# Recurrent heads issued one head ahead of the attention heads in a hybrid decoder block

## Chip, core, metric

The kernel runs on one core of a Trainium2 chip. The metric is the device time of one execution in microseconds (us). It is compared with the kernel before on the same inputs: 1024 tokens, model width 1024, one layer, float32.

## What is computed

One decoder block. The normed input `h` goes through one wide projection; part of it feeds an RWKV-7 recurrence (8 heads of 64), part a differential attention (4 heads, two score maps each), part the two gates of the merge. The merged result passes `w_out`, a residual, and then a PEER expert layer: for each token 128 rows of a table `u` and 128 rows of a table `v` are chosen by product keys.

```python
z = h @ w_in
zs, zq, zk, zv, zg = split(z)
ya = rwkv7_time_mix(token_shift(zs))         # a scan over time, per head
yb = diff_attention(zq, zk, zv)              # (softmax1 - lam*softmax2) @ v, ALiBi, causal
ga, gb = split(zg)
x = x + (sigmoid(ga) * (ya @ proj_a) + sigmoid(gb) * (yb @ proj_b)) @ w_out
h2 = rmsnorm(x)
ids, gates = product_key_topk(h2)            # 128 experts per token
act = gelu(u_tab[ids] . h2) * gates
x = rmsnorm(x + sum(act * v_tab[ids]))
```

## The kernel before

The 1024 tokens are worked in two groups of 512 (`GROUPS`, L25). For each group a generator `mix` (L245) makes the time mixing, the attention, the merge and the residual; `pick` (L679) scores the product keys. The recurrence is done for two RWKV heads at a time, so `rwkv(h)` with h = 0 to 3 is called a recurrent head here. It is written in chunks of 64 tokens: a decay scan (`G`, L304), products per chunk (`MB`, L335), a triangular inverse that goes out to memory and back (`m_s`, `z_s`, L369 to L385, then `XT`, L405), transfer matrices (`Pd`, L440), eight serial state steps (`sn` and `st`, L468 and L469), and the output `ysb`, finished at L482 and stored to `y_s`. `attention(h)` (L508) makes the scores of four tiles of 128 queries, the softmax and the values, and ends with `oT` (L590), also stored to `y_s`. In the second group it reads the first group's keys and values back (`ko`, `vo`, L513). `rkv(h)`, `att_in(h)` and `gate_in(i)` are column blocks of the projection, 24 matmuls each (`z`), whose weights are split into two parts on ACT (`whi`, L154) and DVE (`wlo`, L155). `fill()` (L611) puts gate columns between the attention tiles; `NG` says how many belong to which head.

The merge (L627) reads the eight `y_s` blocks back (`yld`), splits them, and makes for each of eight output blocks `d` the two halves i = 0 (recurrent) and i = 1 (attention): the product with `proj` (`pj`), times the gate (`sgm`), and the sum (`mg`, L643, L645). Then `w_out` and the residual (`x`, L669).

The expert layer is done in two ways. For the first group's four chunks of 128 tokens, `choose` (L712) makes `ids`, and `peer` (L807) gathers the rows: 128 gathers of `u` and 128 of `v` for each chunk, 1024 in all, each a POOL-issued indirect DMA into one of five `uv` buffers and one DVE instruction on 128x1024 elements (L815 or L822). For the second group, `gates` and `ahead` prepare dense gate tables and `dense` (L861) runs through all 128 blocks of 128 experts, here called dense heads: on DVE each has one `gw` multiplication at L885, and the results in PSUM are added up at L926.

All this is handed to a tile scheduler in the order in which it is written: what comes earlier in the text has priority, and the scheduler fixes for each engine one order of instructions before the program runs. The gathers of `peer` are written last (L954), so they fill what the scheduler holds to be free places. On the chip each engine works through its list in that order; an instruction that waits holds back all behind it. The four `choose` calls of the first group are handed over at the `yield`s of the second group's `mix` (L932 to L935, `CHO`).

Of the kernel before, what the change touches and what calls it, by code (L numbers as in the profile page):

```python
# [9 lines left out]
F32R = mybir.dt.float32r  # L10
# [4 lines left out]
OP = mybir.AluOpType  # L15
# [22 lines left out]
NG = (2, 3, 3, 8)  # L38
# [10 lines left out]
def body(ctx: ExitStack, tc: tile.TileContext, ins, out, dbg=None):  # L49
    nc = tc.nc  # L50
# [194 lines left out]
    def mix(gi, t0, W):  # L245
# [241 lines left out]
        def att_in(h):  # L487
            slope = 2.0 ** (-2 * (h + 1))
            b = zt(14 + h)
            qT = at("qT")[:, :W]  # L490
            nc.scalar.activation(qT, b, AF.Copy, scale=0.125 / slope)
            b = zt(18 + h)
            kT = at("kTn")[:, :W]
            nc.scalar.activation(kT, b, AF.Copy)
            b = zt(22 + h)
            t = at("zvT")[:, :W]
            nc.scalar.activation(t, b, AF.Copy)
            b2 = abank("vtr")[:, :W]
            for a in range(TT):
                nc.tensor.transpose(b2[:, a * P:(a + 1) * P], t[:, a * P:(a + 1) * P], ident)  # L500
            vn = at("vn")[:, :W]
            nc.scalar.activation(vn, b2, AF.Copy)
            if t0 + W < T:
                nc.sync.dma_start(ins["k_s"][h, :, t0:t0 + W], kT)
                nc.sync.dma_start(ins["v_s"][h, :, t0:t0 + W], vn)
            return qT, kT, vn

        def attention(h, qT, kT, vn, fill):  # L508
            slope = 2.0 ** (-2 * (h + 1))
            segs = []  # L510
            if t0:
                ko, vo = at("ko")[:, :t0], at("vo")[:, :t0]
# [1 line left out]
                nc.sync.dma_start(vo, ins["v_s"][h, :, 0:t0])  # L514
                segs.append((0, t0, ko, vo))
            segs.append((t0, t0 + W, kT, vn))
            bo = obank("oT")[:, :W]
            def scores(a):

# [82 lines left out]
        nc.scalar.activation(lo_[0:64, :], lo_[0:64, :], AF.Tanh)  # L602
        nc.scalar.activation(gl, gl, AF.Sigmoid)
        show("lora", lo_, (slice(None), slice(t0, t0 + W)))
        zz, q = rkv(0), att_in(0)
        yield
        order = iter(range(16))
        for h in range(4):
            left = [NG[h]]

            def fill():  # L611
                if left[0]:
                    left[0] -= 1
                    gate_in(next(order))

            rwkv(h, *zz)
            if h < 3:
                zz = rkv(h + 1)
            attention(h, *q, fill)
            if h < 3:  # L620
                q = att_in(h + 1)
            while left[0]:
                fill()
            yield


        yh, yl, mcat = [], [], []  # L627
        for k in range(8):
            y = at("yld")[:, :W]
            nc.sync.dma_start(y, ins["y_s"][gi, k, :, :W])  # L630
            yh.append(rt_("yh", F32R))
            yl.append(rt_("yl", F32R))
            split(y, yh[k], yl[k])
        mg = [r2("mg") for _ in range(4)]
        for d in range(8):
            m = []
            for i in range(2):
                sgm = at("sgm")[:, :W]
                nc.sync.dma_start(sgm, ins["g_s"][gi, 8 * i + d, :, :W])
                b = zbank("pj")[:, :W]  # L640
                wmul(b, ins["proj"][d, i:i + 1], lambda k: yh[4 * i + k], lambda k: yl[4 * i + k], 4)
                t = mg[d // 2][:, d % 2 * 512:d % 2 * 512 + W] if i == 0 else sgm
                nc.vector.tensor_tensor(t, sgm, b, op=OP.mult)  # L643
                m.append(t)
            nc.vector.tensor_tensor(m[0], m[0], m[1], op=OP.add)  # L645
            show("mrg", m[0], (d, slice(None), slice(t0, t0 + W)))
            mcat.append(m[0])
        mh, ml = [], []
        for m in mcat:
            mh.append(rt_("mh", F32R))  # L650
# [380 lines left out]
```

## Times and profile before

| | us |
|---|---|
| median of 3 runs (lowest, highest) | 3510.96 (3509.01, 3511.16) |
| the profiled execution, its own time | 3513.99 |
| span of its profile | 3512.2 |
| PE busy in the span | 3085.0 |
| DVE busy | 2876.8 |
| ACT busy | 1412.5 |
| POOL busy | 1334.3 |

The profile is of one execution. Its time is 1.8 us over its span and 3.0 us over the median. PE is TensorE, DVE VectorE, ACT ScalarE, POOL GpSimd; SP issues most DMAs. Matmul ends are modelled, so PE's busy share says less than the distance between the starts of matmuls. The program has stages with different limits, so that shares over the whole span say little and the stretches must be read one by one.

### The profile page before, as it was taken

How to read it: one execution, taken by the hardware profiler on the slowest of the kernel's cores; microseconds unless marked ns; L12 is line 12 of the kernel's file. 1: busy time of each engine (PE TensorE's matmuls, PEld its weight loads, DVE VectorE, ACT ScalarE, POOL GpSimd, SP SyncE). 2: the span in 40 equal slices, each digit the busy share in tenths (PEclk: the TensorE clock that was granted, in tenths of full speed). 3: DMA queues.
4: the chain of work that ended last, by engine and by line, in shares of the span. 5: the costliest groups of instructions: out<-in, count | busy, mean ns of one | idle time of the engine just before them, and what ended most of it. 6: DMA issues, size and time to landing. Idle time of an engine off the chain costs nothing. (4 is left out here: it accounts for less than half of the span.)

```text
span 3512.2 us, 51039 instructions
## 1 busy us (share of the span) xinstructions
PE 3085.0 (88%) x17382; PEld 2404.1 (68%) x17382; DVE 2876.8 (82%) x6546; ACT 1412.5 (40%) x2634; POOL 1334.3 (38%) x1036
## 2 busy tenths in 40 slices
PE   6999998999778965889888689999989999999996
PEld 5777776777555754667666468777767777777775
DVE  4655557977978777999888679998989998988999
ACT  3444434443424331334999543333323333333332
POOL 0000000024553355421122426665555665655664
PEclk9999999998888886999989799999999999999998
DMA  4222454256675688864668999999999999999997
GB/s 128 75 74 72 122 159 160 77 174 220 227 252 185 221 284 291 308 199 133 198 209 276 308 343 343 351 358 350 356 345 345 352 353 349 367 348 339 354 351 279
DMA packets 407525, 898.69 MB, mean 256 GB/s; under 512 B 69024, under 2 KB 140000, under 8 KB 403168
## 3 DMA queue, kind: packets, MB, share of 16 engines
q0 software_dynamic: 147456, 536.94, 43.4%
q1 hardware_dynamic: 259808, 358.49, 30.4%
q8 instruction: 137, 2.24, 0.3%
q14 instruction: 124, 1.02, 0.1%
HBM read 829.22 MB, written 66.07 MB: 255 GB/s over the span
## 5 line engine op out<-in xcount | busy, mean ns | idle before, releaser
L793 POOL DMA_INDIRECT uv<-u,ids x512 | 655.2, 1280 | 1255.3 <-DVE uv L815 626.6
L793 POOL DMA_INDIRECT uv<-v,ids x512 | 677.9, 1324 | 519.2 <-DVE acc L822 372.4
L822 DVE SCALAR_TENSOR_TENSOR acc<-uv,act,acc 128x1024 f32<-128x1024 f32 x512 | 655.4, 1280 | 72.2 <-DMA uv<-v,ids 65.7
L815 DVE SCALAR_TENSOR_TENSOR uv<-uv,hb 128x1024 f32<-128x1024 f32 x512 | 617.4, 1219 | 87.3 <-DMA uv<-u,ids 84.5
L154 ACT ACTIVATE whi<-wraw 128x512 fp32r<-128x512 f32 x552 | 339.0, 627 | 595.2 <-PE z L170 207.1
L155 DVE TENSOR_TENSOR wlo<-wraw,whi 128x512 fp32r<-128x512 f32 x552 | 374.5, 686 | 132.5 <-ACT whi L154 124.9
L169 PE MATMUL ua<-fh,whi 128*128 128x512 f32 x1024 | 419.7, 410 | 61.5 <-ACT ye L905 39.9
L170 PE MATMUL ua<-fl,whi 128*128 128x512 f32 x1024 | 417.3, 408 | 0.0
L176 ACT ACTIVATE ah<-gw 128x512 fp32r<-128x512 f32 x128 | 80.8, 632 | 727.0 <-DVE gw L885 723.1
L180 PE MATMUL yk<-vh,ah 128*128 128x512 f32 x768 | 307.0, 400 | 25.8 <-ACT ah L176 24.8
L182 PE MATMUL yk<-vh,al 128*128 128x512 f32 x768 | 308.3, 401 | 6.8 <-DVE al L177 5.8
L181 PE MATMUL yk<-vl,ah 128*128 128x512 f32 x768 | 306.0, 398 | 5.8 <-DVE vl L177 5.8
L173 PE MATMUL ua<-fh,wlo 128*128 128x512 f32 x1024 | 269.7, 402 | 23.6 <-DVE wlo L155 23.6
L169 PEld LDWEIGHTS ua<-fh,whi 128*128 128x128 f32 x1024 | 201.1, 196 | 112.9 <-ACT ye L905 45.1
L169 PE MATMUL z<-hh,whi 128*128 128x512 f32 x672 | 274.8, 410 | 1.0 <-ACT whi L154 1.0
L173 PE MATMUL z<-hh,wlo 128*128 128x512 f32 x672 | 275.1, 410 | 0.7 <-DVE wlo L155 0.7
L170 PE MATMUL z<-hl,whi 128*128 128x512 f32 x672 | 275.3, 410 | 0.0
L844 PE MATMUL gb<-oh,ohg 128*128 128x128 f32 x1024 | 228.3, 344 | 40.3 <-ACT ohg L843 37.8
L173 PEld LDWEIGHTS ua<-fh,wlo 128*128 128x128 f32 x1024 | 193.5, 191 | 73.0 <-DVE wlo L155 31.4
L844 PEld LDWEIGHTS gb<-oh,ohg 128*128 128x128 f32 x1024 | 168.0, 212 | 103.1 <-ACT ohg L843 64.4
L843 ACT ACTIVATE ohg<-ohb,sl 128x128 f32<-128x128 bf16 x512 | 231.2, 560 | 2.0 <-DVE ohb L838 2.0
L170 PEld LDWEIGHTS ua<-fl,whi 128*128 128x128 f32 x1024 | 201.0, 196 | 44.3
(321 smaller groups left out, 5739.8 us busy)
## 6 DMA issues: line engine op xcount, KB each, us to landing
wraw<-ut SPq DMA_DIRECT2D x256, 256.0 KB
vraw<-v SPq DMA_DIRECT2D x256, 256.0 KB
wraw<-w_in SPq DMA_DIRECT2D x168, 256.0 KB
gd_s<-st SPq DMA_DIRECT2D x16, 2048.0 KB
gt<-gd_s SPq DMA_DIRECT2D x32, 1024.0 KB
wraw<-wq SPq DMA_DIRECT2D x64, 256.0 KB
g_s<-sgo SPq DMA_DIRECT2D x32, 256.0 KB
wraw<-proj SPq DMA_DIRECT2D x32, 256.0 KB
```

What stands on the lines that cost most here:

```text
L154: nc.scalar.activation(hi, raw, AF.Copy)
L155: nc.vector.tensor_tensor(lo, raw, hi.bitcast(F32), op=OP.subtract)
L169: nc.tensor.matmul(o, hi, xh(k), start=(k == 0), stop=False)
L170: nc.tensor.matmul(o, hi, xl(k), start=False, stop=False)
L173: nc.tensor.matmul(o, lo, xh(k), start=False, stop=(k == n - 1))
L180: nc.tensor.matmul(o, ah, bh, start=first, stop=False)
L181: nc.tensor.matmul(o, ah, bl, start=False, stop=False)
L182: nc.tensor.matmul(o, al, bh, start=False, stop=last)
L793: nc.gpsimd.indirect_dma_start(out=t, out_offset=None, in_=ins[src], in_offset=bass.IndirectOffsetOnAxis(ap=ids[:, j:j + 1], axis=0))
L815: nc.vector.scalar_tensor_tensor(u, u, 1.0, hb, op0=OP.mult, op1=OP.mult, accum_out=act[:, j:j + 1])
L822: nc.vector.scalar_tensor_tensor(acc, v, act[:, j:j + 1], acc, op0=OP.mult, op1=OP.add)
L844: nc.tensor.matmul(b[:, k:512:4], o3[:, k], o1[:, k], start=True, stop=True)
```

## The change

Two things are written in another order.

First, the loop over heads runs five times. In round h it hands over `rwkv(h)` and the next head's columns `rkv(h + 1)`, and then the attention of head h - 1 with its gate columns. Before, `rwkv(h)`, `rkv(h + 1)` and `attention(h)` came together, so a recurrent head now stands ahead of the attention of the head before it, and attention 3 with its eight gate columns stands alone at the end. The `yield`s, and with them the `choose` calls, come after attention 0 to 3 as before. The reads of `ko` and `vo` move from `attention` into `att_in`, one head earlier.

Second, the merge takes the half i = 0 of all eight blocks first, with the four recurrent `yld` blocks, and then the half i = 1 with the four of the attention. The same products and sums are made; nothing is added or left out.

```diff
@@ -503,10 +503,6 @@
             if t0 + W < T:
                 nc.sync.dma_start(ins["k_s"][h, :, t0:t0 + W], kT)
                 nc.sync.dma_start(ins["v_s"][h, :, t0:t0 + W], vn)
-            return qT, kT, vn
-
-        def attention(h, qT, kT, vn, fill):
-            slope = 2.0 ** (-2 * (h + 1))
             segs = []
             if t0:
                 ko, vo = at("ko")[:, :t0], at("vo")[:, :t0]
@@ -514,6 +510,10 @@
                 nc.sync.dma_start(vo, ins["v_s"][h, :, 0:t0])
                 segs.append((0, t0, ko, vo))
             segs.append((t0, t0 + W, kT, vn))
+            return qT, segs
+
+        def attention(h, qT, segs, fill):
+            slope = 2.0 ** (-2 * (h + 1))
             bo = obank("oT")[:, :W]
             def scores(a):
 
@@ -602,49 +602,55 @@
         nc.scalar.activation(lo_[0:64, :], lo_[0:64, :], AF.Tanh)
         nc.scalar.activation(gl, gl, AF.Sigmoid)
         show("lora", lo_, (slice(None), slice(t0, t0 + W)))
+
         zz, q = rkv(0), att_in(0)
         yield
         order = iter(range(16))
-        for h in range(4):
-            left = [NG[h]]
-
-            def fill():
-                if left[0]:
-                    left[0] -= 1
-                    gate_in(next(order))
-
-            rwkv(h, *zz)
+        left = [0]
+
+        def fill():
+            if left[0]:
+                left[0] -= 1
+                gate_in(next(order))
+
+        for h in range(5):
+            if h < 4:
+                rwkv(h, *zz)
             if h < 3:
                 zz = rkv(h + 1)
-            attention(h, *q, fill)
-            if h < 3:
-                q = att_in(h + 1)
-            while left[0]:
-                fill()
-            yield
+            if h:
+                left[0] = NG[h - 1]
+                attention(h - 1, *q, fill)
+                if h < 4:
+                    q = att_in(h)
+                while left[0]:
+                    fill()
+            if h:
+                yield
 
 
         yh, yl, mcat = [], [], []
-        for k in range(8):
-            y = at("yld")[:, :W]
-            nc.sync.dma_start(y, ins["y_s"][gi, k, :, :W])
-            yh.append(rt_("yh", F32R))
-            yl.append(rt_("yl", F32R))
-            split(y, yh[k], yl[k])
         mg = [r2("mg") for _ in range(4)]
-        for d in range(8):
-            m = []
-            for i in range(2):
+        for i in range(2):
+            for k in range(4 * i, 4 * i + 4):
+                y = at("yld")[:, :W]
+                nc.sync.dma_start(y, ins["y_s"][gi, k, :, :W])
+                yh.append(rt_("yh", F32R))
+                yl.append(rt_("yl", F32R))
+                split(y, yh[k], yl[k])
+            for d in range(8):
                 sgm = at("sgm")[:, :W]
                 nc.sync.dma_start(sgm, ins["g_s"][gi, 8 * i + d, :, :W])
                 b = zbank("pj")[:, :W]
                 wmul(b, ins["proj"][d, i:i + 1], lambda k: yh[4 * i + k], lambda k: yl[4 * i + k], 4)
-                t = mg[d // 2][:, d % 2 * 512:d % 2 * 512 + W] if i == 0 else sgm
-                nc.vector.tensor_tensor(t, sgm, b, op=OP.mult)
-                m.append(t)
-            nc.vector.tensor_tensor(m[0], m[0], m[1], op=OP.add)
-            show("mrg", m[0], (d, slice(None), slice(t0, t0 + W)))
-            mcat.append(m[0])
+                m = mg[d // 2][:, d % 2 * 512:d % 2 * 512 + W]
+                if i == 0:
+                    nc.vector.tensor_tensor(m, sgm, b, op=OP.mult)
+                    continue
+                nc.vector.tensor_tensor(sgm, sgm, b, op=OP.mult)
+                nc.vector.tensor_tensor(m, m, sgm, op=OP.add)
+                show("mrg", m, (d, slice(None), slice(t0, t0 + W)))
+                mcat.append(m)
         mh, ml = [], []
         for m in mcat:
             mh.append(rt_("mh", F32R))
```

What the scheduler makes of it is read from the orders of the two programs. `z` is a column block of the projection, `bg` the last product of a recurrent head, `am` the first products of the next one; lines behind L602 stand six lines later in the changed program.

**PE, first group, between recurrent heads 0 and 1.** Before, from `bg` of head 0 on, columns of the projection stand between all steps of the next head; the piece begins

```order
L481 MATMUL bg<-gl,lora 128x512
L589 MATMUL hb<-ident,rsw 128x128
L173 MATMUL z<-hh,wlo 128x512
L169 MATMUL z<-hh,whi 128x512
L170 MATMUL z<-hl,whi 128x512
```

and now

```order
L481 MATMUL bg<-gl,lora 128x512
L235 MATMUL hs<-blk,sq 128x2 x4
L242 MATMUL hb<-ident,rb 128x128 x4
L289 MATMUL bu<-wlal,lora 128x512
L293 MATMUL ba<-wlal,lora 128x512
L318 MATMUL bb<-av,blk 128x512
L332 MATMUL am<-KR,bT 64x128 x16
L332 MATMUL am<-KR,kT 64x128 x16
```

From `Pd` of head 0 to `am` of head 1 there were 109 matmuls of `z` (36 up to `bg`, 38 up to `bu`, 35 up to `am`); now there are none. They stand behind the last recurrent head instead: between its `bg` and the first `w_out` product there were 17, now 166.

**DVE, second group, end of recurrent head 3.** Before, `ysb` of head 3 and `oT` of attention 3 stood side by side, and the merge followed:

```order
L590 SCALAR_TENSOR_TENSOR oT<-oT,sub_105,hb 128x512
L482 TENSOR_TENSOR ysb<-ysb,bg 128x512
L177 TENSOR_TENSOR yl<-yld,yh 128x512
L822 SCALAR_TENSOR_TENSOR acc<-uv,act,acc 128x1024 x5
L177 TENSOR_TENSOR yl<-yld,yh 128x512
L822 SCALAR_TENSOR_TENSOR acc<-uv,act,acc 128x1024
```

Now this `oT` is that of attention 2, and the choice of the last chunk, gate columns and gathers follow:

```order
L590 SCALAR_TENSOR_TENSOR oT<-oT,sub_105,hb 128x512
L482 TENSOR_TENSOR ysb<-ysb,bg 128x512
L750 CAST d_11708<-ch 128x128
L828 SCALAR_TENSOR_TENSOR acc<-uv,act,acc 128x1024
L751 TENSOR_SCALAR d_11708<-d_11708 128x128
L155 TENSOR_TENSOR wlo<-wraw,whi 128x512
L752 SCALAR_TENSOR_TENSOR d_11708<-d_11708 128x128
```

Attention 3 and its gate columns come after that, ahead of the merge. Counted on DVE in the two orders, the gathers that stand ahead of certain places are:

| gathers ahead of | before | changed |
|---|---|---|
| first `ids` of the second group's mix | 0 | 0 |
| `ysb` of recurrent head 3 | 215 | 219 |
| first `mg` of the merge | 221 | 251 |
| first residual `x` | 255 | 282 |
| first dense head | 366 | 395 |
| dense head 64 | 667 | 694 |
| dense head 124 of 0 to 127 | 998 | 1024 |
| first `accd` (L926) | 1019 | 1024 |

**DVE, end of the program.** Before, gathers stand among the last sums:

```order
L822 SCALAR_TENSOR_TENSOR acc<-uv,act,acc 128x1024
L926 TENSOR_TENSOR accd<-accd,yk 128x512
L822 SCALAR_TENSOR_TENSOR acc<-uv,act,acc 128x1024
L926 TENSOR_TENSOR accd<-accd,yk 128x512 x5
L822 SCALAR_TENSOR_TENSOR acc<-uv,act,acc 128x1024
L907 TENSOR_TENSOR accd<-accd,ye 128x512 x2
```

and now the last four dense heads and the sums stand without any:

```order
L891 TENSOR_TENSOR gw<-gw,gt 128x512
L177 TENSOR_TENSOR al<-gw,ah 128x512
L913 TENSOR_TENSOR accd<-accd,ye 128x512
L177 TENSOR_TENSOR vl<-vraw,vh 128x512
L913 TENSOR_TENSOR accd<-accd,ye 128x512
L932 TENSOR_TENSOR accd<-accd,yk 128x512 x6
```

## Rows read from the trace of the kernel before

**Rows 1.** Page, part 4: the chain that ended last, by engine.
```profile
issue 20%; POOL 15%; DMA 7%; ACT 2%; DVE 1%; PE 1%; POOLq 0%; DVEq 0%; ACTq 0%
```

**Rows 2.** Windows: us, busy of PE, PEld, DVE, ACT, POOL (instructions), PE clock, DMA share, GB/s.
```profile
94.00:449.00 355.00, 349.28 (x3608) 263.71 (x3607) 208.63 (x671) 164.57 (x294) 0.46 (x4) 0.99 0.29 86
...
145.00:194.00 49.00, 46.74 (x451) 34.85 (x442) 28.88 (x94) 19.64 (x34) 0.11 (x1) 0.97 0.22 71
...
750.00:908.00 158.00, 128.51 (x1058) 95.15 (x1058) 135.15 (x402) 54.42 (x91) 75.49 (x59) 0.82 0.72 237
908.00:1070.00 162.00, 127.20 (x1072) 95.25 (x1072) 136.22 (x396) 57.11 (x94) 82.36 (x58) 0.85 0.70 229
1070.00:1235.00 165.00, 149.45 (x1161) 116.44 (x1162) 129.96 (x353) 69.21 (x111) 61.17 (x47) 0.89 0.64 207
1235.00:1369.00 134.00, 80.16 (x883) 63.80 (x882) 107.35 (x188) 31.78 (x59) 76.00 (x60) 0.75 0.82 279
1369.00:1475.00 106.00, 89.02 (x362) 68.81 (x361) 90.56 (x108) 26.19 (x43) 44.66 (x38) 0.92 0.91 316
...
2026.00:3430.00 1404.00, 1323.74 (x5533) 1051.48 (x5534) 1267.64 (x1761) 461.34 (x839) 819.39 (x625) 0.98 0.96 350
3430.00:3484.00 54.00, 51.27 (x213) 40.73 (x213) 52.04 (x58) 14.45 (x26) 35.16 (x29) 0.97 0.86 295
```

**Rows 3.** Timeline of DVE, first group: start us, us, instruction [idle before].
```profile
145.31 0.42 DVE L440 TENSOR_TENSOR Pd<-Pp,eyec 128x256 f32<-128x256 f32 x1 [2.67 <-PE Pp L430]
...
193.75 0.69 DVE L335 TENSOR_TENSOR MB<-am,mask 128x512 f32<-128x512 f32 x1 [0.22 <-PE am L332]
...
448.44 0.68 DVE L482 TENSOR_TENSOR ysb<-ysb,bg 128x512 f32<-128x512 f32 x1
...
460.75 0.68 DVE L643 TENSOR_TENSOR mg<-sgm,pj 128x512 f32<-128x512 f32 x1
...
543.40 0.68 DVE L669 TENSOR_TENSOR x<-x,xo 128x512 f32<-128x512 f32 x1
```

**Rows 4.** Timeline of PE, first group: five projection matmuls in a row, first and last.
```profile
83.72 0.39 PE L170 MATMUL z<-hl,whi 128*128 128x512 f32 x1
...
84.63 0.39 PE L173 MATMUL z<-hh,wlo 128*128 128x512 f32 x1
```

**Rows 5.** Timeline of DVE, second group: recurrent head 3, first merge sum, first residual.
```profile
1368.50 0.68 DVE L482 TENSOR_TENSOR ysb<-ysb,bg 128x512 f32<-128x512 f32 x1
...
1387.80 0.69 DVE L643 TENSOR_TENSOR mg<-sgm,pj 128x512 f32<-128x512 f32 x1 [3.32 <-DMA sgm<-g_s]
...
1475.35 0.68 DVE L669 TENSOR_TENSOR x<-x,xo 128x512 f32<-128x512 f32 x1
```

**Rows 6.** Groups of DVE, 750 to 1475 us: busy us, mean ns | idle before.
```profile
L822 DVE SCALAR_TENSOR_TENSOR acc<-uv,act,acc 128x1024 f32<-128x1024 f32 x127 | 162.5, 1279 | 18.4 <-DMA uv<-v,ids 17.5
L815 DVE SCALAR_TENSOR_TENSOR uv<-uv,hb 128x1024 f32<-128x1024 f32 x128 | 154.6, 1215 | 8.6 <-DMA uv<-u,ids 8.6
...
L815 DVE DVE_READ_ACCUMULATOR uv<-uv,hb 128x1 f32 x128 | 10.2, 80 | 0.0
```

**Rows 7.** Waits of DVE and PE, 700 to 1480 us: us in total, times, longest us.
```profile
DVE yl L177 <- ACT yh L176: 5.7, 1, 5.7
...
DVE mg L643 <- DMA sgm<-g_s: 3.3, 1, 3.3
...
PE sc L528 <- DMA ko<-k_s: 18.7, 3, 8.3
```

**Rows 8.** Timeline of DVE, end: `gw` of dense head 124, first sum, last gathered row.
```profile
3443.46 0.68 DVE L885 TENSOR_TENSOR gw<-gw,gt 128x512 f32<-128x512 f32 x1
...
3483.52 0.68 DVE L926 TENSOR_TENSOR accd<-accd,yk 128x512 f32<-128x512 f32 x1
...
3493.47 1.28 DVE L822 SCALAR_TENSOR_TENSOR acc<-uv,act,acc 128x1024 f32<-128x1024 f32 x1
```

**Rows 9.** Page, part 3: the queue of the 1024 gathers: packets, MB, share.
```profile
q0 software_dynamic: 147456, 536.94, 43.4%
```

## Prediction

> **What bounds the kernel now.** I read the chain of waits first. It ends in the gathers: "issue" and POOL hold a third of the span, and no other engine comes near [rows 1]. That says where the program ends, not what each stage waits for, so I went on to the windows, cut at the places that the order names [rows 2].
>
> The reader is to see three regimes there. In the first group's heads (94 to 449 us) PE is busy for 349.28 of 355 us at a clock of 0.99, and there are no gathers: PE is the limit. In the second group's mix (750 to 1475 us) the granted clock falls to between 0.75 and 0.92 (means of its two levels, 1.2 and 2.4 GHz) and PE has gaps. DVE, which now also carries the gathers, is busy for 135.15 + 136.22 + 129.96 + 107.35 + 90.56 = 599.2 of 725 us; 125.8 us are idle. It is nearest to the limit, held back by the recurrence. From 2026 us on (dense heads beside gathers) the DMA engines are busy for 0.96 at 350 GB/s and DVE for 1267.64 of 1404 us: this stage is full.
>
> The time at the end is therefore the start of the dense stage plus what that stage has left. The change can act on the first group's mix, on the second group's mix, and on the tail through the gathers that the mixes leave over.
>
> **First group.** No work is added. What moves is the filling: between `Pd` of head 0 and `am` of head 1 there were 109 projection matmuls and now there are none. That stretch took 193.75 - 145.31 = 48.4 us [rows 3], and PE was busy for 46.74 of 49 us there [rows 2]. Five projection matmuls in a row start 0.91 us apart from first to last, so one costs 0.91 / 4 = 0.23 us [rows 4]; 109 of them are 25 us. If the steps of the recurrence are quick without them, the stretch takes 48.4 - 25 = 23 us and the 25 us are paid later: a sum of 0. If the recurrence itself needs the 48 us, 25 us are added. On the other side, `ysb` of head 3 and the first merge sum stood 460.75 - 448.44 = 12.3 us apart [rows 3], a wait for stores and reads back, which 166 matmuls now cover. The term lies between -12 and +25 us. I take 0, because the row of that stretch shows PE full and not waiting.
>
> **Second group.** DVE carries the same instructions as before and more gathers: 282 instead of 255 stand ahead of the first residual, 27 more. One is a row of `v` at 1.28 us and 26 are rows of `u` at 1.215 + 0.080 us [rows 6], together 1.28 + 26 x 1.295 = 35 us. If the idle time stays at 125.8 us, the stretch grows by 35 us. Two waits go, since the recurrent half of the merge finds its inputs stored long before: `yl` 5.7 and `mg` 3.3 us, 9 us in all [rows 7]. The earlier reads of `ko` and `vo` take three PE waits of 18.7 us away [rows 7]; I cost that at nothing, as DVE and not PE is the fuller engine in this stretch. If that cover goes, they are a gain of up to 18.7 us. The two reads stand earlier on SP's queue; they are the same 256 KB each, and two more buffers are held for one head. The gap of 1387.80 - 1368.50 = 19 us ahead of the merge [rows 5] is filled by the choice of the last chunk, gate columns and attention 3, which were ahead of it before: work moved, not saved. The eight gate columns and their `wlo` move with it, at the same count.
>
> So the term is +35 - 9 = +26 us. The bounds: all 27 gathers fall into idle time, -9 us; or the idle share becomes that of the worst quarter, 1070 to 1235 us, with 35.0 of 165 us idle [rows 2]: (599.2 + 35) / 0.788 = 805 us, +80 us. The best quarter (22.9 of 158 us idle) gives 742 us, +17 us. I take +26 us, near the best quarter.
>
> **From the residual to the dense heads.** 111 gathers stood in it, now 113: the same work, hidden in the same places. I cost it at 0; two gathers more would be 2.6 us.
>
> **Tail.** By bytes it should shrink a lot. A gather moves 536.94 / 1024 = 0.524 MB [rows 9], 29 fewer are 15.2 MB, and at 350 GB/s that is 43 us. But the order does not let the tail run ahead. Up to dense head 124 it holds 998 - 366 = 632 gathers before and 1024 - 395 = 629 now, at the same steady mixture. Three gathers less are -4 us. Only the last four dense heads lose theirs. They took 3483.52 - 3443.46 = 40 us [rows 8], with DVE busy for 52.04 of 54 us and 213 matmuls starting in that time [rows 2]. Without 21 gathers DVE has 27 us less to do, PE is next, and 213 x 0.23 = 49 us instead of 54 make 4 us of the 40. After the first `accd` five gathers go, 5 x 1.28 = -6 us. Together -14 us. Bounds: -37 us if DVE alone set the end (29 x 1.28), 0 if the closing stores do.
>
> The DMA share is 0.64 to 0.91 in the mix and 0.96 in the tail [rows 2], and the change moves gathers from the fuller stage into the less full one; were the tail paid by bytes, the sum would be 0 + 26 - 43 = -17 us. That is a rival below. The Trainium skill, page Perfetto Trace Analysis, section Optimization Strategy, speaks for that rival: a kernel whose contended engine changes from stage to stage may gain when the stages are interleaved. By the rule this change should gain; by the counts of the order the tail keeps its pace and the sum stays at +12 us.
>
> **Sum.** 0 + 26 + 0 - 14 = +12 us on the profiled execution's 3513.99 us. That execution is 3.0 us over the median of the runs, so against 3510.96 us the forecast is 3523 us, slower by 0.3%. About 0.2%, 7 us, is what a measurement of this kernel can tell from no change.
>
> **The rivals.**
>
> *The mix swallows the gathers (faster).* The place is DVE between 750 and 1475 us. It has 125.8 us of idle time, and the recurrence, now ahead of the attention, leaves gaps of its own for gathers. If all 27 fall into them, the mix changes by -9 and the tail by -14: 3488 us. For it: 98.8 of the 125.8 us of idle time are other waits than those for gathers, mostly on steps of the recurrence, and a gather that has landed could run in them. Against it: DVE works in a fixed order, and the other 18.4 + 8.6 = 27.0 us come just before gathers, waiting for their landing [rows 6]; a gather put into the recurrence can also be late. It decides from the point at which more than 19 of the 35 us are swallowed (35 - 9 - 19 = 7 against -14 in the tail). Chance 0.25.
>
> *The tail pays by bytes (faster).* If the steady part runs quicker with fewer bytes left, it gives 43 us: 0 + 26 - 43 = -17, 3494 us. Against it stand the counts up to dense head 124. Chance 0.06.
>
> *The two cancel (no change).* The mix grows by about as much as the end loses, around 14 us: 3511 us. Chance 0.15. That the change does nothing, because the scheduler undoes it, is nearly ruled out by the orders; chance 0.02, same time.
>
> *The recurrence starves (much slower).* Head 0 and the start of head 1 stand nearly alone, and the whole mix falls to the worst quarter's share: +80 - 14 = +66, 3577 us. For it: 1235 to 1369 us, where recurrent head 3 stood nearly alone, has PE busy for 80.16 of 134 us at a clock of 0.75 [rows 2]. Against it: that place is filled now. Chance 0.12.
>
> *Forecast.* 0.40.
>
> **The numbers.** Slower 0.40 + 0.12 = 0.52, same 0.15 + 0.02 = 0.17, faster 0.25 + 0.06 = 0.31. Cases of both signs hold most of the chance. The forecast's own range is 3513 to 3545 us: the first group at -10 to +10 and the mix at its best quarter or some 20 us worse. The range for 8 in 10 takes in the first faster case at its centre and half of the way to the worst one: 3487 to 3562 us.
>
> **What would show it.** In the changed profile the first residual `x` of the first group stands at 543 us [rows 3] within 12, that of the second near 1500 instead of 1475 us, and DVE is busy some 35 us longer between. The first dense `gw` comes some 26 us late, dense head 124 about 1414 us after it as before (3443 - 2026 = 1417), and no `acc` row stands among the `accd` rows. I am wrong if the second residual is at or before 1475 us (the mix swallowed the gathers), if the stretch from the first `gw` to head 124 is clearly shorter (bytes decide), or if the first group moves by more than 15 us either way.

## Result: 1.5% slower, four times the forecast loss

| | before | changed |
|---|---|---|
| median (lowest to highest), us | 3510.36 (3509.01 to 3511.16), 4 runs | 3563.82 (3559.85 to 3569.24), 4 runs |
| profiled execution, us | 3513.99 | 3559.85 |
| span of its profile, us | 3512.2 | 3558.1 |

The ratio is 1.0154, with a 95% interval of 1.0136 to 1.0171: 53 us slower. The forecast was 12 us slower, its range ended at 3562 us. The two profiles differ by 45.9 us of span. The changed kernel's profile is of its fastest run, 4.0 us under its median, and the one of before lay 3.6 us over its own: 45.9 + 4.0 + 3.6 = 53.5.

The profile after is read in the order of the prediction. On the page, the chain of waits still ends in the gathers [rows 1]:

```profile
issue 16%; POOL 12%; DMA 9%; PE 3%; DVE 2%; ACT 0%; SPq 0%; POOLq 0%; DVEq 0%; ACTq 0%
```

DVE's timeline after the change has these starts (us, duration, instruction; x2 where two stand back to back): `Pd` of head 0, `MB` of head 1, `ysb` of head 3, first merge sum, first residual; the last three again for the second group; then `gw` of dense head 124 and the first `accd` [rows 3, 5, 8].

```profile
145.86 0.75 DVE L440 TENSOR_TENSOR Pd<-Pp,eyec 128x256 f32<-128x256 f32 x2 [2.67 <-PE Pp L430]
189.89 1.29 DVE L335 TENSOR_TENSOR MB<-am,mask 128x512 f32<-128x512 f32 x2 [1.24 <-PE am L332]
427.99 0.68 DVE L482 TENSOR_TENSOR ysb<-ysb,bg 128x512 f32<-128x512 f32 x1
480.85 0.68 DVE L648 TENSOR_TENSOR mg<-sgm,pj 128x512 f32<-128x512 f32 x1
562.75 1.28 DVE L675 TENSOR_TENSOR x<-x,xo 128x512 f32<-128x512 f32 x2
...
1352.73 0.68 DVE L482 TENSOR_TENSOR ysb<-ysb,bg 128x512 f32<-128x512 f32 x1
1443.49 0.68 DVE L648 TENSOR_TENSOR mg<-sgm,pj 128x512 f32<-128x512 f32 x1
1532.85 0.69 DVE L675 TENSOR_TENSOR x<-x,xo 128x512 f32<-128x512 f32 x1
...
3495.97 0.68 DVE L891 TENSOR_TENSOR gw<-gw,gt 128x512 f32<-128x512 f32 x1
3530.61 1.38 DVE L932 TENSOR_TENSOR accd<-accd,yk 128x512 f32<-128x512 f32 x2 [1.48 <-PE yk L182]
```

The first residual is 19.4 us late (562.75 against 543.40), the second 57.5 (1532.85 against 1475.35), dense head 124 is 52.5 late (3443.46 before), and the first last sum 47.1 (3483.52 before). So the first group lost 19, the second group's mix 38 (4 of it before the first `ids`, which starts at 748 before and at 772 now), and what follows gave 10 back.

The windows of the same stretches (us, busy of PE, PEld, DVE, ACT, POOL, PE clock, DMA share, GB/s), the first group first, then mix, pick and tail:

```profile
145.90:190.00 44.10, 24.30 (x310) 17.99 (x312) 21.00 (x63) 11.41 (x18) 0.11 (x1) 0.62 0.02 7
...
428.00:481.00 53.00, 53.00 (x237) 39.53 (x236) 25.55 (x72) 28.90 (x54) 0.00 (x0) 1.00 0.69 234
481.00:563.00 82.00, 82.00 (x353) 65.52 (x352) 41.14 (x65) 24.22 (x39) 0.00 (x0) 1.00 0.41 129
...
771.00:1533.00 762.00, 584.28 (x4533) 448.74 (x4534) 635.45 (x1515) 227.86 (x386) 382.32 (x288) 0.83 0.76 257
...
1533.00:1727.00 194.00, 154.86 (x702) 122.62 (x702) 186.95 (x823) 62.39 (x110) 45.18 (x41) 0.89 0.61 203
2093.00:3490.00 1397.00, 1328.52 (x5560) 1057.94 (x5561) 1272.82 (x1750) 466.81 (x846) 802.90 (x624) 0.97 0.96 353
```

and of before, for the stretch from `ysb` of head 3 to the first merge sum in the first group, for the mix, and for the stretch from the second residual to the gates:

```profile
448.00:461.00 13.00, 8.02 (x27) 5.87 (x27) 6.52 (x11) 5.17 (x9) 0.00 (x0) 0.82 0.82 266
...
748.00:1475.00 727.00, 574.83 (x4535) 439.76 (x4536) 601.24 (x1448) 240.14 (x398) 340.70 (x261) 0.85 0.74 247
...
1475.00:1656.00 181.00, 154.13 (x701) 120.38 (x700) 176.05 (x815) 64.98 (x114) 35.45 (x31) 0.92 0.60 193
```

Three things are to be seen. In the first row PE is busy for 24.3 of 44.1 us, where it was busy for 46.74 of 49 before [rows 2]: the projection matmuls are gone and the stretch hardly got shorter (44.0 us from `Pd` to `MB` in place of 48.4). In the mix DVE is busy 34.2 us longer (635.45 against 601.24) in a stretch 35 us longer: its idle time stayed (126.6 against 125.8). From the residual to the gates there are 13 us more, with DVE busy for 187 of 194. From the gates to the first `gw` it is 367 us against 370.

The mix's longer DVE time is gathers, 282 in place of 255 (fields behind the bar: busy us, mean ns, idle before) [rows 6]:

```profile
L821 DVE SCALAR_TENSOR_TENSOR uv<-uv,hb 128x1024 f32<-128x1024 f32 x154 | 186.3, 1218 | 31.8 <-DMA uv<-u,ids 31.1 <-issue 0.3
L828 DVE SCALAR_TENSOR_TENSOR acc<-uv,act,acc 128x1024 f32<-128x1024 f32 x128 | 163.4, 1277 | 9.5 <-DMA uv<-v,ids 6.1 <-issue 2.7
```

### The profile page after: what moved, and what is told of

Read it like the earlier page. It is cut to its first block, busy times and chain, and to the rows that moved or that the text cites. A ratio compares the mean times of both kernels' runs of the same rounds, so it can differ in the third digit from the quotient of the medians.

```text
span 3558.1 us, 51092 instructions
## 1 busy us (share of the span) xinstructions
PE 3095.2 (87%) x17382; PEld 2417.6 (68%) x17382; DVE 2887.0 (81%) x6546; ACT 1395.9 (39%) x2618; POOL 1320.4 (37%) x1036
## 3 DMA queue, kind: packets, MB, share of 16 engines
q14 instruction: 127, 1.03, 0.1%
## 5 line engine op out<-in xcount | busy, mean ns | idle before, releaser
L799 POOL DMA_INDIRECT uv<-v,ids x512 | 665.0, 1299 | 609.5 <-DVE acc L828 414.3
```

What stands on the lines that cost most here:

```text
L799: nc.gpsimd.indirect_dma_start(out=t, out_offset=None, in_=ins[src], in_offset=bass.IndirectOffsetOnAxis(ap=ids[:, j:j + 1], axis=0))
```

## Experiments

The theory after the result had two parts. The recurrence of the first group has nothing beside it between heads 0 and 1, and the projection columns that used to stand there are now paid in front of the merge. And the second group pays for gathers that now stand ahead of its residual. The first rival put the cost on the other edits (the halved merge, the earlier reads of `ko` and `vo`); the second on SP, where the residual's reads of `x` now wait in front of the merge's reads. All kernels were run beside the kernel before on the same chip; in these sets of runs (on four chips) it took 3486 to 3494 us, and in the set of the result, whose chip is not known, 3510. So only ratios and distances inside one profile are compared. Each profile is of one execution.

This table has the DVE starts of every profile, in us from the start of the span (group 1: `ysb` of head 3, first merge sum, residual; first `ids`; group 2: residual; first `gw`; first `accd`), the mix (first `ids` to second residual), the tail (first `gw` to first `accd`), what follows to the end, and from the orders the gathers ahead of the second residual, of the first `gw` and of the first `accd`.

| kernel | ysb | mg | x | ids | x | mix | gw | accd | tail | end | gathers |
|---|---|---|---|---|---|---|---|---|---|---|---|
| before | 448 | 461 | 543 | 748 | 1475 | 727 | 2026 | 3484 | 1458 | 29 | 255, 366, 1019 |
| changed | 428 | 481 | 563 | 772 | 1533 | 761 | 2093 | 3531 | 1437 | 27 | 282, 395, 1024 |
| e1_merge_only | 448 | 458 | 539 | 747 | 1464 | 717 | 2014 | 3467 | 1453 | 29 | 256, 367, 1019 |
| e2_loop_only | 429 | 482 | 564 | 772 | 1536 | 764 | 2096 | 3539 | 1443 | 28 | 291, 395, 1024 |
| e3_first_group | 428 | 482 | 563 | 772 | 1503 | 731 | 2065 | 3521 | 1456 | 26 | 257, 380, 1024 |
| e4_second_group | 447 | 458 | 539 | 748 | 1511 | 763 | 2068 | 3525 | 1458 | 29 | 282, 395, 1024 |
| e5_before_no_gather | 447 | 459 | 541 | 752 | 1310 | 558 | 1818 | 3154 | 1336 | 28 | none |
| e6_changed_no_gather | 428 | 481 | 563 | 776 | 1337 | 560 | 1843 | 3179 | 1337 | 28 | none |
| e7_x_later | 424 | 477 | 559 | 767 | 1523 | 756 | 2078 | 3515 | 1437 | 28 | 282, 395, 1024 |
| e8_fill4 | 429 | 469 | 551 | 759 | 1546 | 787 | 2099 | 3541 | 1442 | 28 | 289, 395, 1024 |
| e9_fill_first | 427 | 467 | 549 | 758 | 1511 | 753 | 2067 | 3513 | 1446 | 28 | 282, 395, 1024 |
| e11_choose_later | 429 | 482 | 564 | 943 | 1409 | 466 | 1970 | 3435 | 1465 | 182 | 162, 270, 929 |
| e12_before_choose_later | 447 | 458 | 541 | 858 | 1389 | 531 | 1952 | 3420 | 1467 | 135 | 180, 297, 955 |
| e13_last_choice_later | 445 | 457 | 539 | 745 | 1414 | 669 | 1980 | 3441 | 1460 | 43 | 237, 359, 1011 |

In the rows of e11 and e12 the first `ids` itself comes later, so there the second residual is compared and not the mix.

How far such a distance can be trusted is seen in the changed kernel, e4, e7 and e9: from the first `ids` to the end their DVE works through the same instructions in the same order, and yet the mix takes 753 to 763 us, the stretch from the residual to `gw` 555 to 561 and the tail 1437 to 1458. In the old order of the second group (before, e1, e3) the mix takes 717 to 731 us.

**The parts of the change.** The halved merge and the early reads alone, in the loop of before:

```diff
-        for h in range(5):
...
+        for h in range(4):
...
+            rwkv(h, *zz)
             if h < 3:
                 zz = rkv(h + 1)
...
+            attention(h, *q, fill)
```

> The loop over heads as before, the merge in halves and the earlier ko and vo reads as in the changed kernel. Theory (the loop costs the time: a starved recurrence in the first group, more gathers on DVE in the second): within 7 us of the kernel before, since 256 gathers stand ahead of the second residual instead of 255. Rival (the halved merge and its place on SP's queue cost the time): 30 to 55 us slower than before, with the first merge sum of the second group more than 30 us behind the last recurrent output.

Measured: 3498.24 against 3486.15 us, ratio 1.0025 (1.0004 to 1.0046), 9 us by the mean of the ratio and 12 by the medians, a little over the 7 allowed. In its profile the second mix takes 717 us and 256 gathers stand ahead of the residual, so there is no loss in the mixes; where the 9 us are is not settled. The rival of the merge, 30 to 55 us, falls.

The new loop alone, with the merge of before (the cut is against the changed kernel):

```diff
-        for i in range(2):
-            for k in range(4 * i, 4 * i + 4):
...
+        for k in range(8):
+            y = at("yld")[:, :W]
```

> The new loop over heads with the merge block by block as before. Theory (the loop): 40 to 60 us slower than the kernel before, as the changed kernel; the first residual of the first group near 563 us. Rival (the halved merge): at most 20 us slower.

Measured: 3568.8 against 3486.15 us, ratio 1.0233 (1.0188 to 1.0278). That is 83 us, above the numbers of both theories. With e1 beside it on the same chip, the loop carries the cost and the halved merge does not add to it. In this order 291 gathers stand ahead of the second residual.

**One group at a time.** The new loop and merge in one group, the old ones in the other; this is e3, and e4 has `gi == 1`:

```diff
+        if gi == 0:
...
+        else:
```

> The change in the first group of 512 tokens alone. Theory (two separate costs): 12 to 22 us slower than the kernel before: the first residual of the first group at 563 us instead of 543, the rest as before. Rival (the gathers of the second group are the whole cost): within 7 us.

> The change in the second group alone. Theory (two separate costs): 25 to 38 us slower than the kernel before, the first residual of the first group at 543 us, the stretch from the first chosen ids to the second residual near 760 us instead of 727, the tail some 20 us shorter. Rival (the gathers are the whole cost): 45 to 55 us slower.

Measured: 1.0149 (1.0099 to 1.0199) for the first group and 1.0158 (1.0119 to 1.0197) for the second, some 52 and 55 us. Both were over the numbers of the theory, and the second lies at those of its rival, so the two times by themselves do not tell the parts from each other; the table and the next experiment do.

For the first group, against e1 on the same chip, its first residual is 24 us late as expected. But the unchanged second group's mix takes 731 in place of 717 us with one gather more, and 13 more are lost between the residual and `gw`, where 123 gathers stand (257 to 380) in place of 111 (256 to 367). The 13 have a reason in the counts: the scheduler, whose plan for the first group is another one, has put the gathers of the second group at other places too, though that group is written as before. The 15 in the mix have not: they are mostly idle time of DVE (127 us in place of 116), which is 126 in the kernel before.

For the second group the first residual of the first group is at 539 us, as in e1, and the mix is at 763 us as expected. The 20 us that the tail was to give back did not come (1458 us). So the costs of the groups do not add up: e3 and e4 together would cost more than the whole.

**Without gathers.** Both kernels without the first group's expert sums, one run each:

```diff
     def peer(bi, ids, gate):
...
-        for j in range(P):
-            u = gather("u", ids, j)
...
-        for j in range(P):
-            v = gather("v", ids, j)
...
         finish(acc, rows, pp_, "uv", NU)
```

> The kernel before without the 1024 gathers and their DVE instructions: the first group's expert sums are left out. It is the base for the next run: its stretch from the first chosen ids to the second residual. If gathers and their waits set that stretch, it falls from 727 us to below 560; if PE and the recurrence set it, it stays above 620.

> The changed kernel without the gathers, the same part left out. Theory (the extra gathers cost the second group its 34 us): the stretch from the first chosen ids to the second residual is within 12 us of the run before it. Rival (the recurrence, left without filling at the start, and attention 3 with its gates at the end cost it): 25 to 45 us longer than the run before it, without any gather. In both cases the first residual of the first group comes near 563 us instead of 543.

Measured: 3184.45 and 3208.87 us. The windows of the two mixes, from the first `ids` to the second residual, before and changed, columns as above:

```profile
752.00:1310.00 558.00, 535.41 (x4535) 409.46 (x4536) 324.69 (x1066) 235.89 (x394) 0.34 (x3) 0.95 0.26 81
```

```profile
776.00:1337.00 561.00, 524.08 (x4537) 406.85 (x4538) 324.91 (x1063) 232.80 (x389) 0.23 (x2) 0.95 0.26 80
```

The mix of before falls from 727 to 558 us, just under the 560 that were to show that the gathers set it. The two mixes are equal within 3 us: without gathers the second group loses nothing by the new order, and PE is the limit in both (535 and 524 us busy at a clock of 0.95). The rival asked for 25 to 45 us. Since PE and not DVE is the limit here, this does not exclude that the new order makes DVE wait more where DVE is the limit. That is answered by DVE's idle time in the mixes with gathers: 116 to 127 us in the old order (e1, before, e3) and 119 to 129 in the new one (e9, e7, changed, e4). The 24 us between the two kernels are those up to the first `ids` (752 and 776 us), where no kernel has gathers. This separates the two parts: the first group's loss is the recurrence and PE, the second's is the gathers.

**SP's queue.** In the changed profile SP waits at the residual's `x` loads while the last attention still holds their buffers, and the merge's reads stand behind them. This is the wait view of SP from 1340 to 1450 us (in total, times, longest):

```profile
SPq L663 <- PE pT L562: 31.9, 2, 26.2
```

An edit that writes these loads behind `w_out`:

```diff
-            nc.sync.dma_start(x1[a], ins["x"][t0 + a * P:t0 + (a + 1) * P, :])
         banks = [f("xo") for f in (zbank, zbank, rbank, rbank, rbank, abank, abank, obank)[:2 * TT]]
...
+            nc.sync.dma_start(x1[a], ins["x"][t0 + a * P:t0 + (a + 1) * P, :])
```

> The changed kernel with the reads of x for the residual written behind the w_out products, so that they don't stand ahead of the merge's reads on SP's queue, where they waited up to 26 us for the attention's buffers. Theory (that wait delays the merge of the second group): from the last recurrent output to the first merge sum 65 to 80 us instead of 91, the whole kernel 8 to 25 us faster than the changed one (1.008 to 1.014 of the kernel before where that one has 1.0154). Rival (DVE has the choice of the last chunk and the gathers to do in that time anyway): the same time as the changed kernel within 6 us.

Measured: 3557.08 against 3487.54 us, 1.0209 (1.0186 to 1.0232). The scheduler put these loads at the same place on SP as before and left the orders of PE, DVE, ACT and POOL as they were, so the question wasn't asked; on SP two neighbouring reads, one of `nw` and one of `w_out`, changed places. The run is worth something else: it is nearly the changed kernel once more in another set of runs, where it costs 1.0209 and not 1.0154. Buffers of their own for `x` were not tried, so what the wait costs stays open.

**Cover for the first group.** Four of the eight gate columns of the last attention are handed over between recurrent heads 0 and 1, in both groups (e8, shown), and in the first alone (e9, with `and gi == 0`):

```diff
-NG = (2, 3, 3, 8)
+NG = (2, 3, 3, 4)
...
                 zz = rkv(h + 1)
+            if h == 0:
+                for _ in range(4):
+                    gate_in(next(order))
```

> The changed kernel with four of the eight last gate columns handed over between recurrent heads 0 and 1, in both groups. Theory (the first group loses 20 us because nothing fills PE between heads 0 and 1, and the columns are paid at the end): the first residual of the first group at 540 to 549 us instead of 563, the whole 12 to 24 us faster than the changed kernel. Rival (attention 3 alone at the end costs it, whatever fills the start): the first residual stays within 6 us of 563.

> The changed kernel with four of the last eight gate columns handed over between recurrent heads 0 and 1, in the first group only; the second group's order stays as in the changed kernel (251 gathers ahead of the merge, 282 ahead of the residual, 395 ahead of the dense heads). Theory (the first group pays because PE starves between heads 0 and 1 and the columns left over stand in front of the merge): the first residual comes at 551 instead of 563 us, and the whole is 10 to 14 us faster than the changed kernel, so a ratio to the kernel before near 1.0175 where the changed kernel's order gave 1.0209. Rival (the first group's delay is paid back by the gathers, which then find other places): the second group's mix takes over 770 instead of 762 us and the whole stays at 1.021.

Measured: e8 1.0253 (1.0222 to 1.0283), e9 1.0149 (1.0123 to 1.0176). The first residual came at 551 and 549 us, 12 and 14 earlier than in the changed kernel: with four columns handed over earlier, 12 to 14 of the 20 us are back (540 to 549 us were expected of e8). The window from `Pd` of head 0 to `MB` of head 1 in e8:

```profile
142.27:184.92 42.65, 34.60 (x359) 24.29 (x361) 27.32 (x84) 14.86 (x30) 0.11 (x1) 0.89 0.15 51
```

Of the four columns 66 matmuls stand in it, 15 us at 0.23 us each, and it takes 42.65 us where it took 44.0 without any and 48.4 with 109 (42.5 in e9). So the steps of the recurrence need some 43 us there, and 66 matmuls in their waits cost nothing.

In the second group the same edit does harm: the mix grows to 787 us, with 289 gathers ahead of its residual and 144 us of idle time on DVE, and the whole is 13 us slower than e7 on the same chip (3570 against 3557 us) where 12 to 24 us less were expected. In e9 the second group's order is untouched (282, 395) and its mix is 753 us. Its ratio is under that of e7 and about that of the changed kernel itself; it did not run beside either, so a gain in the whole is likely by the profile but not shown.

**What a gather costs where.** If the second group's cost is the place of the gathers, then putting fewer of them into the mix should give it back, unless they cost as much elsewhere. Each choice of experts is handed over one `yield` later, in the changed kernel (e11) and in the kernel before (e12):

```diff
-CHO = (1, 1, 1, 1, 0)
+CHO = (0, 1, 1, 1, 1)
```

> The changed kernel with each choice of the first group's experts handed over one yield later: 162 instead of 282 gathers stand ahead of the second residual, 270 instead of 395 ahead of the dense heads, and 929 instead of 1024 ahead of the last sums. Theory (a gather in the second group's mix costs 0.6 to 1.3 us there, one in the tail or behind it as much): the mix falls from 762 to between 610 and 690 us, the tail from the first dense head to the first sum and the end behind it together grow by 100 to 160 us, and the whole is within 40 us of the changed kernel. Rival (gathers are dear in the mix and cheap in the tail, so that the change lost only because it moved them the wrong way): the tail grows by less than 70 us and the whole is faster than the kernel before.

> The kernel before with the same edit, each choice one yield later: 180 instead of 255 gathers ahead of the second residual, 297 instead of 366 ahead of the dense heads, 955 instead of 1019 ahead of the last sums. Theory (equal prices in the mix and in the tail): the mix falls from 727 by 50 to 95 us, the tail and the end grow by 60 to 100 us, the whole is within 30 us of the kernel before. Rival (cheap in the tail): the whole is faster than the kernel before by 20 us or more.

Measured: 1.035 (1.0313 to 1.0387) and 1.0175 (1.0147 to 1.0203), both slower than their own base. The second residual moved as the theory says: in e12 by 86 us (1475 to 1389) for 75 gathers, 1.15 us each; in e11 by 124 (1533 to 1409) for 120, 1.03 us each. Both theories had the price of a gather the same in the tail, both rivals had it cheap there and the whole faster. The whole was slower, and more than the theories allowed; the tail and the end together grew by 116 us in e12, where 60 to 100 were expected. But the tail itself took hardly more gathers than before: 1467 us with 658 gathers between the first `gw` and the first `accd` in e12 (e11: 1465 with 659), against 1458 with 653 before. What was left fell behind the last sums. A window there in e12, and DVE's largest group from the first `accd` to the end (3420 to 3555 us):

```profile
3445.00:3545.00 100.00, 0.00 (x0) 0.00 (x0) 78.60 (x91) 2.30 (x4) 64.92 (x54) 0.50 0.91 322
```

```profile
L822 DVE SCALAR_TENSOR_TENSOR acc<-uv,act,acc 128x1024 f32<-128x1024 f32 x69 | 88.6, 1283 | 25.1 <-DMA uv<-v,ids 24.1
```

69 gathers stand alone behind the sums, PE has nothing to do, and the end is 135 us behind the first `accd` in place of 29. One costs (135 - 29) / (69 - 5) = 1.66 us there. In the second group's mix one gather more or less costs 1.0 to 1.15 us, by the two distances above.

In the tail the 653 gathers of before cost 1458 - 1336 = 122 us in all, 0.19 us each, by e5 (one run, of another set). That is an average, and the average of the 255 in the mix by the same run is (727 - 558) / 255 = 0.66 us, also less than one more of them costs. What one more costs in the tail is less sure. The six kernels with 629 gathers in it, in one and the same DVE order (changed, e2, e4, e7, e8, e9), take 1437 to 1458 us, the five with 652 to 659 (before, e1, e11, e12, e13) 1453 to 1467. By the means, 1444 and 1461 us, that is an estimate of some 0.65 us each, with a spread of 21 us in one order, more than the 17 between the means. And the tail takes some 5 for each dense head and not more than 659 in any order built.

This tells what the change did: its tail holds 1024 - 395 = 629 gathers, 24 fewer than before, so it gave up places in the tail and paid more for them in the mix and the pick. How much more for one gather is not settled.

The same prices ask for a kernel with a few fewer gathers in the mix than before and not many behind the sums. Handing over the last choice alone one `yield` later gives 237, 359 and 1011 in the kernel before:

```diff
-CHO = (1, 1, 1, 1, 0)
+CHO = (1, 1, 1, 0, 1)
```

> The kernel before with the last of the four choices alone one yield later: 237 instead of 255 gathers ahead of the second residual, and 13 instead of 5 behind the first of the last sums. By the prices of the two runs with all choices later (about 1.15 us for a gather in the second group's mix, about 1.7 us for one behind the sums) the mix falls by 18 x 1.15 = 21 us, the end grows by 8 x 1.7 = 14 us, and the whole is some 7 us faster than the kernel before. Rival (the place of the choice itself costs as much, or the closing stores no longer cover the gathers behind the sums): same or slower.

Measured: 3478.82 against 3494.35 us, ratio 0.9957 (0.994 to 0.9973), 15 us faster than the kernel before, in one set of runs on one chip. The end grew by 14 us as expected (29 to 43). The mix fell by more than 21 us: by 58 against the kernel before, whose profile is from the set with 3510 us, and by 48 against e1. The stretch from the residual to `gw` grew by 16, with 39 gathers up to the gates (237 to 276) in place of 28 (255 to 283). Its mix in two windows, cut at `ysb` of head 3:

```profile
745.00:1312.00 567.00, 465.53 (x4172) 351.50 (x4173) 488.38 (x1324) 215.27 (x355) 273.48 (x206) 0.88 0.73 243
1312.00:1414.00 102.00, 91.39 (x370) 70.83 (x369) 90.44 (x108) 26.42 (x43) 44.44 (x38) 0.93 0.91 326
```

DVE is busy for 578.8 us, 22 less than before, which are the 18 gathers; its idle time is 90 us in place of 126 (116 in e1). That second part was not foreseen. It lies between `ysb` of heads 2 and 3, 129 us (1183 to 1312) in place of 165 (1204 to 1369; 169 in e1). Why DVE waits less there is not settled; one part is seen in the groups, the state steps' wait for `sn`:

```profile
L469 DVE SCALAR_TENSOR_TENSOR st<-sn,G,Qm 128x64 f32<-128x64 f32 x28 | 7.8, 280 | 3.4 <-PE sn L468 3.2
```

It was 18.2 us before:

```profile
L469 DVE SCALAR_TENSOR_TENSOR st<-sn,G,Qm 128x64 f32<-128x64 f32 x28 | 7.9, 282 | 18.2 <-PE sn L468 16.7 <-PE y L430 1.4
```

## Why the prediction was right in its sign and four times too small

**First group: 0 forecast, +19 measured, 4 more up to the first `ids`.** This is the step that failed: "If the steps of the recurrence are quick without them, the stretch takes 48.4 - 25 = 23 us and the 25 us are paid later: a sum of 0", taken "because the row of that stretch shows PE full and not waiting". The stretch takes 189.89 - 145.86 = 44 us. So 109 matmuls cost some 4 us there and not 25; the others stood in the waits of the recurrence, and PE was busy because they filled them. PE's longest waits in the first group's heads are now for its own chain (in total, times, longest):

```profile
PE bb L318 <- DVE kz L270: 11.7, 2, 10.3
PE hb L242 <- ACT rb L239: 6.9, 2, 3.7
```

A part of the 44 us is the clock. With PE idle for 20 of them the granted clock fell from 0.97 [rows 2] to 0.62, and the matmuls that stayed got longer; the product `bu` (L289) takes 1138 ns on the mean of two where it took 641. By an estimate from the mean lengths of all that stand in both stretches this is at most some 9 us of PE's busy time. It is not the main part: with 66 matmuls put back (e8) the clock is 0.89, and the stretch takes 42.65 us, only 1.4 less.

The upper bound of +25 was that case, and the text priced it; a busy engine was taken as proof that it sets the pace. The side for the better was wrong too. The 12.3 us between `ysb` of head 3 and the first merge sum were read as a wait, but PE was busy for 8.02 of 13 us there, so 5 us were free. The 166 matmuls do stand in that place now, and it takes 52.9 us with PE full (53.00 of 53). e6 shows the same 563 us without any gather, and e8 and e9 give 12 to 14 us back by filling the hole.

**Second group: +26 forecast, +34 measured.** The mechanism is the one forecast: DVE in order, 27 gathers, no idle time swallowed (DVE busy +34.2 us, idle 125.8 and 126.6), and without gathers (e6) the new order costs nothing. That the idle times agree within 1 us is luck, as they spread over 116 to 129 us in both orders. What failed is the credit "Two waits go ... 9 us in all". Of the two, `mg`'s 3.3 us went and `yl`'s 5.7 became 4.0, but waits for gathers grew by more: 18.4 + 8.6 = 27.0 us of idle time before them in the old order [rows 6], 31.8 + 9.5 = 41.3 now.

**Residual to dense heads: 0 forecast, +10 measured.** "111 gathers stood in it, now 113: the same work, hidden in the same places." The count was taken over the whole stretch. Up to the gates it was 28 (255 to 283) and is 40 (282 to 322), and there DVE has nothing to hide them in: 176 of 181 us busy before. The twelve cost 13 us. Behind the gates ten fewer give back 3. The same is seen in e3 and e13, with 39 up to the gates in each; in the same order in other sets of runs (e4, e7, e9) the whole stretch takes 5 to 6 us more and not 10.

**Tail: -14 forecast, -22 in this profile.** From the first `gw` to head 124 it is 1402.5 us where it was 1417.6, against -4 forecast, and 35 from there to the first sum where it was 40, as forecast. The -6 us for five gathers behind the first `accd` did not come: from there to the end it is 27.5 us where it was 28.7. The forecast for the last four heads set the 40 us of [rows 8] beside a row of 54 us; cut at head 124, DVE was busy for 39.14 of 41 us and PE for 38.27. And e4, with DVE's order the same, takes 1422 us up to head 124 and 1458 in the tail, no less than before. So this gain is not sure.

Sum of the profile: 19.4 + 4.0 + 34.2 + 10.1 - 20.6 - 1.2 = +45.9.

**The rivals.** *The mix swallows the gathers* falls by the unchanged idle time. *The tail pays by bytes* asked for 43 us and is at -15 up to head 124 at best, within the spread of 1402 to 1422 us of one order. The Trainium skill (Perfetto Trace Analysis, Optimization Strategy) says that interleaving regimes may improve performance. In this step it did not: 29 gathers moved out of a stage with a DMA share of 0.96 into stages with 0.60 to 0.76, and that cost 34 + 10 us against the 22 of the tail. *The recurrence starves* had its mechanism in the right hole, heads 0 and 1, but I priced it in the second group alone; it was the first group that starved, and there it cost 19 us.

Of the marks named beforehand, two came: DVE busy +34 for 35, and no `acc` row among the last sums. The second residual stands at 1533 us and not near 1500, the first `gw` comes 68 us late and not 26, and head 124 stands 1402 us behind it and not 1414. The first residual came 19 us late, more than the 12 allowed to it and the 15 that were to count against the forecast.

## What to carry to other kernels

A stretch in which an engine is full does not tell how long the work without its filling would take: look for the chain under it, and as long as its length is not known, the bound against the change belongs in the sum, not only in the range. In a program with fixed orders, background work has a price for each place, and a stage had a fixed number of places here: count it stage by stage, as far as the stages have different limits, before saying that it is the same. The average price in a stage is not the price of one more. And a change to one stage moves the background work of all the later ones, so parts that are tried alone do not add up.

## What the runs showed of the hardware

Gathers alone are not bound by DVE. In e12's window of 100 us with no matmul POOL issued 54 of them, one each 1.85 us, with the DMA engines at 0.91 and 322 GB/s and DVE busy for 78.6: dearer than the 1.28 us that DVE needs for one. In the tail, beside PE at a clock of 0.97 to 0.98, one cost 0.19 us on the average, and by an estimate from eleven profiles some 0.65 us on the margin.

In the hole between heads 0 and 1 the mean granted clock was 0.62, between the two levels (1.2 and 2.4 GHz), with PE busy for 24.3 of 44.1 us. With 66 matmuls more (e8) it was 0.89, with 109 (before) 0.97 [rows 2]. With no matmul at all (e12 above) it was 0.50, the lower level.

Nearly the same two programs differ by 1.0154 in one set of runs and by 1.0209 (e7) in another, where only two neighbouring reads on SP stand the other way round; the intervals, 1.0136 to 1.0171 and 1.0186 to 1.0232, do not meet. The kernel before took 3486, 3488, 3492 and 3494 us on four chips and 3510 in the set of the result. What makes the sets differ is not settled, but an interval from one set does not hold for the next.
